# A batched matrix product: stores issued two at a time behind every second load of x

## The chip, the cores and the metric

The kernel runs on one core of a Trainium2 chip. A core has five engines that run at the same time and wait for one another by semaphores: PE (TensorE, matrix products), DVE (VectorE), ACT (ScalarE), POOL (GpSimd) and SP (SyncE). Sixteen DMA engines move data between the chip's main memory (DRAM) and the core's working memory; DMAs issued by POOL go to one queue (q0 below), those issued by SP to another (q1). The metric is the time of one execution in microseconds (us). "Span" is the time from the first to the last instruction in a profiled execution.

## The reference

```
batch, m, k, n = 32, 512, 1024, 768
x:      (batch, m, k)  float32
weight: (batch, k, n)  float32
out = np.matmul(x, weight).astype(np.float32)      # (32, 512, 768)
```

Thirty-two independent products of a 512x1024 and a 1024x768 matrix. 168 MB are read and 50 MB written.

## The kernel before

The batches go two by two: 16 pairs (`PAIRS`). Both inputs are cast to bf16 by the DMA that loads them, except for the first x, which SP loads as it is. For every pair k there are these pieces of work:

- **load of x**, x(k) (`load_x`, L108 to L111): 4 MB read, into one of two buffers. POOL first waits until the first quarter batch of products of pair k-2 is done, since the buffer is then free.
- **load of weights**, w(k) (`load_w`, L93 to L102): 6 MB read, both batches with one DMA, into one of two pairs of slots. POOL first waits until all products of pair k-2 are done. The last two batches (30 and 31) are loaded one by one, each behind its own wait.
- **transposes on PE** (L174): x has to be turned so that its columns lie on the partitions. Two bf16 numbers are turned at a time, as one float32; VectorE copies the result out of the accumulator (L220).
- **products on PE** (L166 and L139): per batch four quarters of 128 rows, each of 8 steps with two products. Before a pair's products PE waits for the weights (L178, by the word that SP passes on in `landed`).
- **copies out** of the accumulators by ACT (L262, L266) and VectorE (L271, L273) into one of four out slots (`OUT_SLOTS`). Two sets of accumulators take turns. Before the first copy of pair a, ACT waits in `slot_free` (L231 to L234) until the store of pair a-4 has landed, and passes that word on to VectorE. PE needs the first copies of a batch before its fourth quarter.
- **store**, s(a) (`store`, L117 to L119): 3 MB written. POOL first waits until all copies of pair a are done. The last two pairs are stored by SP: s(14) with one DMA, pair 15 in four half stores (L124).

What sets the order of the transfers is POOL's list, written out in `on_pool`. POOL works through it in order, so an issue stands behind the waits of everything ahead of it; and the queue q0 carries out what is issued in that order. After the first loads, turn k of the loop (k from 0 to 13) issues x(k+2), then s(k-2), then w(k+2). The last two of POOL's stores, s(12) and s(13), follow the loop.

Of the kernel before, what the change touches and what calls it, by code (L numbers as in the profile page):

```python
# [12 lines left out]
def kernel(  # L13
# [16 lines left out]
    PAIRS = B // 2  # L30
    HELD = 2
    GROUPS = 2 * MT
    W_SLOTS, X_SLOTS, OUT_SLOTS = 4, 2, 4

    pe, dve, act, pool, sp = nc.tensor, nc.vector, nc.scalar, nc.gpsimd, nc.sync
# [25 lines left out]
    def sem(name):  # L61
        sems.append(nc.alloc_semaphore(name))
        return sems[-1]
# [8 lines left out]
    s_st = [sem(f"s_st{i}") for i in range(OUT_SLOTS)]  # L72
# [3 lines left out]
    def mm_done(b):  # L76
        return 4 * (b + 1)
# [12 lines left out]
    def together(b):  # L90
        return W_SLOTS <= b < B - 2

    def load_w(b):  # L93
        if together(b):
            if b % 2 == 0:
                pool.wait_ge(s_mm, mm_done(b + 1 - W_SLOTS))
                slots = all_ws[:, b // 2 % 2].rearrange("p r ko n -> p r (ko n)")
                pool.dma_start(out=slots, in_=w_two_view[b // 2]).then_inc(s_w[b % W_SLOTS], 16)  # L98
            return
        if b >= W_SLOTS:  # L100
            pool.wait_ge(s_mm, mm_done(b - W_SLOTS))
        pool.dma_start(out=ws[b % W_SLOTS], in_=w_view[b]).then_inc(s_w[b % W_SLOTS], 16)  # L102
# [5 lines left out]
    def load_x(k):  # L108
        if k >= X_SLOTS:
            pool.wait_ge(s_mm, mm_begun(k - X_SLOTS))  # L110
        pool.dma_start(out=xs[k % X_SLOTS], in_=x_view[k]).then_inc(s_x[k % X_SLOTS], 16)  # L111

    def copied(eng, j):
        eng.wait_ge(s_ap, j + 1)
        eng.wait_ge(s_dp, j + 1)

    def store(eng, a, sem):  # L117
        copied(eng, 4 * a + 3)
        eng.dma_start(out=two_view[a], in_=outs[a % OUT_SLOTS]).then_inc(sem, 16)  # L119
# [222 lines left out]
    def on_pool():  # L342
        load_w(0)
        pool.memset(ident, 0.0).then_inc(s_zero, 1)  # L344
        pool.wait_ge(s_zero, 1)
        pool.affine_select(  # L346
            out=ident,
            in_=ident,
            compare_op=mybir.AluOpType.not_equal,
            fill=1.0,  # L350
            base=0,
            pattern=[[-1, P]],
            channel_multiplier=1,
        ).then_inc(s_ident, 1)
        load_w(1)
        load_x(1)
        load_w(2)
        load_w(3)
        for k in range(PAIRS - 2):
            load_x(k + 2)  # L360
            if k >= 2:
                store(pool, k - 2, s_st[(k - 2) % OUT_SLOTS])
            load_w(2 * k + 4)
            load_w(2 * k + 5)
        for a in range(PAIRS - 2 - HELD, PAIRS - 2):
            store(pool, a, s_st[a % OUT_SLOTS])

    def on_sp():
        for b in range(B):
# [18 lines left out]
    with tc.tile_critical(sync_engine=mybir.EngineType.Activation, no_gpsimd_drain=True):  # L388
        sp.dma_start(x_first, x_view[0]).then_inc(s_first, 16)
        on_pool()  # L390
        on_pe()
        on_dve()
        on_act()
        on_sp()
        clear_on_pool()
# [30 lines left out]
```

## Time and profile before

| | |
|---|---|
| median of 3 runs | 514.0 us (513.78 to 514.5) |
| the profiled execution's own time | 513.18 us |
| its span | 511.1 us |
| PE busy | 433.1 us, 85% |
| DVE / ACT / POOL busy | 42% / 23% / 6% |
| q0 (POOL's DMAs), share of the 16 engines' span | 95.5% |
| q1 (SP's DMAs) | 5.0% |
| DRAM read and written | 167.77 MB and 50.33 MB, 427 GB/s over the span |
| mean granted clock of PE | 0.955 |

How to read a profile: a row of the groups or of the timeline gives the line of the kernel, the engine, the operation and, as `out<-in`, what it writes and reads. A row of the waits has the waiting engine, tile and line, an arrow, what ended the wait, and then the total in us, how often, and the longest. In the timeline the first two numbers are start and duration in us, and in brackets stands the idle time of the engine before it and what ended that. In the slices, each digit is the busy share of a fortieth of the span in tenths. The windows view gives for each stretch of time the busy time of PE, PE's weight loads, DVE, ACT and POOL, then the granted clock of PE, the mean busy share of the DMA engines, and what they moved in GB/s. The trace also has a record of every packet that a DMA engine moved: its start, duration and size.

### The profile page before, as it was taken

To read this page: it belongs to the slowest core of one execution; us is meant where nothing else is said; L and a number is where in the kernel's file an instruction comes from. 1 tells how busy PE (TensorE), PEld (TensorE's weight loads), DVE (VectorE), ACT (ScalarE), POOL (GpSimd) and SP (SyncE) were. 2 spreads that over 40 slices of the span, in tenths; PEclk is the share of its full clock that TensorE was granted. 3 is DMA by queue.
4 is the path that set the end of the run, shared out by engine and by line. 5 is a ranking of instruction groups with operands and counts; after the bars stand their busy time and mean duration, and the time that the engine had idled before them with its cause. 6 is when DMAs were issued, how large, how long until landed. Compare 5 with 4: busy or idle time off the path is not lost. (4 is left out here: it accounts for less than half of the span.)

```text
span 511.1 us, 5831 instructions
## 1 busy us (share of the span) xinstructions
PE 433.1 (85%) x2560; PEld 174.0 (34%) x1536; DVE 212.9 (42%) x332; ACT 116.4 (23%) x197; POOL 29.1 (6%) x54
## 2 busy tenths in 40 slices
PE   0299999999998986969989599896998969889990
PEld 0143435252524341342433324233242333423420
DVE  0343636454536352352443535335353353623631
ACT  1313131313231311302223031130322303123130
POOL 2000001010100000000000000000000001000000
PEclk9999999999999998988999799897998989989996
DMA  8999999999999999999999999999999999999997
GB/s 296 263 210 215 223 213 215 219 299 248 224 330 224 318 231 222 334 223 335 215 237 318 219 337 217 253 304 219 336 215 265 291 222 334 220 272 279 344 435 296
DMA packets 9443, 136.34 MB, mean 267 GB/s; under 512 B 864, under 2 KB 864, under 8 KB 1376
## 3 DMA queue, kind: packets, MB, share of 16 engines
q0 software_dynamic: 8576, 125.83, 95.5%
q1 hardware_dynamic: 864, 10.49, 5.0%
q14 instruction: 3, 0.02, 0.0%
HBM read 167.77 MB, written 50.33 MB: 427 GB/s over the span
## 5 line engine op out<-in xcount | busy, mean ns | idle before, releaser
L166 PE MATMUL pm<-w,xT 128*128 x1024 | 349.1, 392 | 31.8 <-PEq L178 29.5
L139 PE MATMUL pm<-w,xT 128*128 x1024 | 286.2, 279 | 0.0
L166 PEld LDWEIGHTS pm<-w,xT 128*128 128x128 bf16 x1024 | 102.8, 100 | 275.0 <-issue 274.4
L271 DVE COPY outs<-pm 64x512 f32<-64x512 f32 x128 | 88.2, 689 | 200.8 <-DVEq L269 199.4
L262 ACT COPY outs<-pm 64x512 f32<-64x512 f32 x128 | 74.2, 580 | 267.2 <-PE pm L139 266.4
L174 PE MATMUL pt<-ident,x 128*128 128x128 f32 x512 | 84.9, 309 | 33.0 <-PEq L178 22.8
L220 DVE COPY xT<-pt 128x1024 bf16<-128x1024 bf16 x120 | 77.7, 687 | 63.8 <-PE pt L174 63.5
L174 PEld LDWEIGHTS pt<-ident,x 128*128 128x128 f32 x512 | 71.5, 210 | 48.4 <-issue 26.2
L266 ACT COPY outs<-pm 64x512 f32<-64x512 f32 x64 | 37.0, 579 | 97.7 <-PE pm L139 97.7
L273 DVE COPY outs<-pm 64x512 f32<-64x512 f32 x64 | 43.9, 686 | 0.0
L98 POOL DMA_DIRECT2D w<-in_weight_dram x13 | 9.2, 706 | 224.6 <-PE pm L139 224.6
L111 POOL DMA_DIRECT2D x<-in_x_dram x15 | 8.3, 555 | 170.0 <-PE pm L139 147.0
L281 DVE CAST x<-outs 128x1024 bf16<-128x1024 f32 x4 | 2.5, 688 | 18.5 <-DMA outs<-in_x_dram 18.5
L119 POOL DMA_DIRECT2D out_dram<-outs x14 | 7.5, 539 | 8.0 <-DVE outs L273 7.7
L281 ACT CAST x<-outs 128x1024 bf16<-128x1024 f32 x4 | 3.9, 1041 | 16.2 <-DMA outs<-in_x_dram 16.2
L228 DVE COPY xT<-pt 128x512 bf16<-128x512 bf16 x16 | 5.7, 417 | 4.1 <-PE pt L174 4.1
L102 POOL DMA_DIRECT2D w<-in_weight_dram x6 | 3.4, 566 | 17.4 <-PE pm L139 16.2
L281 ACT ACT_TABLE_LOAD x1 | 1.3, 1283 | 1.0 <-ACTq L388 1.0
L346 POOL TENSOR_SCALAR_AFFINE_SELECT ident<-ident 128x128 f32<-128x128 f32 x1 | 0.3, 284 | 0.2 <-POOL ident L344 0.2
L344 POOL MEMSET ident<- 128x128 f32 x1 | 0.2, 225 | 0.0
L410 POOL MEMSET const-float32-0.0<- 128x1 f32 x1 | 0.1, 99 | 0.2 <-issue 0.2
L410 POOL MEMSET const-bfloat16-1.0<- 128x1 bf16 x1 | 0.1, 103 | 0.0
(2 smaller groups left out, 0.2 us busy)
## 6 DMA issues: line engine op xcount, KB each, us to landing
out_dram<-outs POOLq DMA_DIRECT2D x14, 3072.0 KB, 43.2
w<-in_weight_dram POOLq DMA_DIRECT2D x13, 3072.0 KB, 39.2
x<-in_x_dram POOLq DMA_DIRECT2D x15, 2048.0 KB, 35.9
w<-in_weight_dram POOLq DMA_DIRECT2D x6, 1536.0 KB, 40.5
outs<-in_x_dram SPq DMA_DIRECT2D x1, 4096.0 KB, 17.6
out_dram<-outs SPq DMA_DIRECT2D x1, 3072.0 KB, 18.7
out_dram<-outs SPq DMA_DIRECT2D x4, 768.0 KB, 14.1
```

The lines of the kernel that those rows point to most:

```text
L98: pool.dma_start(out=slots, in_=w_two_view[b // 2]).then_inc(s_w[b % W_SLOTS], 16)
L111: pool.dma_start(out=xs[k % X_SLOTS], in_=x_view[k]).then_inc(s_x[k % X_SLOTS], 16)
L119: eng.dma_start(out=two_view[a], in_=outs[a % OUT_SLOTS]).then_inc(sem, 16)
L139: return pe.add_instruction(mybir.InstMatmult(name=nc.get_next_instruction_name(), engine=mybir.EngineType.PE, ins=[pe.lower_ap(moving), p ...
L166: last = pe.matmul(*args, start=(ko == 0), stop=(ko == KT - 1))
L174: last = pe.transpose(pts[g % 2][:, j, :], words[:, mo, j::JT], ident)
L220: return dve.tensor_copy(both[g // 2][:, :, :, g % 2].rearrange("p b j i r -> p j b i r"), pt)
L262: last = act.copy(*piece)
L266: act.copy(*pieces(b, p, 2)[0]).then_inc(s_ap, 1)
L271: last = dve.tensor_copy(*piece)
L273: dve.tensor_copy(*pieces(b, p, 2)[1]).then_inc(s_dp, 1)
L281: last = copy(xs[0][:, mo], x_first[:, mo])
```

## The change

In POOL's loop the store of one pair per turn becomes two stores in every second turn. In turn k, if k is even, s(k-3) and s(k-2) follow x(k+2); if k is odd, no store is issued. Turn 2 issues s(0) alone, turns 4, 6, 8, 10 and 12 issue s(1) and s(2), s(3) and s(4), and so on to s(9) and s(10). What is left after the loop, s(11), s(12) and s(13), is issued behind the last weight loads. So every even store keeps its place, and every odd one is issued one turn later; s(11) moves from turn 13 to behind w(30) and w(31). Nothing else is changed: not the waits in `store`, not the four out slots, not the stores of the last two pairs on SP.

```
+        def stores(first, last):
+            for a in range(max(first, 0), last):
+                store(pool, a, s_st[a % OUT_SLOTS])
+
+
         for k in range(PAIRS - 2):
             load_x(k + 2)
-            if k >= 2:
-                store(pool, k - 2, s_st[(k - 2) % OUT_SLOTS])
+            if k % 2 == 0:
+                stores(k - 3, k - 1)
             load_w(2 * k + 4)
             load_w(2 * k + 5)
-        for a in range(PAIRS - 2 - HELD, PAIRS - 2):
-            store(pool, a, s_st[a % OUT_SLOTS])
+        stores(PAIRS - 3 - HELD, PAIRS - 2)
```

## The prediction

> Below, pair k is batches 2k and 2k+1 (k from 0 to 15); x(k), w(k) and s(k) are its load of x, its load of weights and its store. Results are for the profiled execution: it took 513.18 us, 2.1 more than its span of 511.1, and lies 0.8 under the median of 514.0.
>
> **What bounds the kernel now.** I read the slices first, then the queues, the waits, the issue times, and the last microseconds.
>
> ```profile
> span 511.1 us, 5831 instructions
> ...
> DMA  8999999999999999999999999999999999999997
> ...
> q0 software_dynamic: 8576, 125.83, 95.5%
> q1 hardware_dynamic: 864, 10.49, 5.0%
> ```
>
> The 16 DMA engines are busy in every slice, and the two queues' packets add up to the whole span. TensorE is busy for 85%. What it waits for:
>
> ```profile
> ACT outs L262 <- PE pm L139: 266.4, 64, 14.7
> ...
> PE pm L166 <- PEq L178: 29.5, 9, 4.9
> ```
>
> L178 is the wait for a weight load: nine pairs stand up to 4.9 us before their first product. ACT's copies wait for TensorE alone: no row has them waiting for a store, so the wait for a free out slot is never felt. One turn of GpSimd's issues, and the landing of each (issue rows of windows around it: 36.0 us for x, 42.8 for the store, 39.2 for the weights):
>
> ```profile
> 359.21 0.56 POOL L111 DMA_DIRECT2D x<-in_x_dram  x1 [13.62 <-PE pm L139]
> 359.76 0.54 POOL L119 DMA_DIRECT2D out_dram<-outs  x1
> 377.74 0.71 POOL L98 DMA_DIRECT2D w<-in_weight_dram  x1 [17.44 <-PE pm L139]
> ```
>
> A transfer lands some 40 us after its issue, longer than a turn of 31.5: the queue is never empty, and a transfer lands when all before it have. The end, by windows (last three columns: clock, DMA share, GB/s):
>
> ```profile
> 504.00:507.00 3.00, 0.00 (x0) 0.00 (x0) 0.00 (x0) 0.00 (x0) 0.00 (x0) 0.50 1.02 426
> 507.00:508.00 1.00, 0.00 (x0) 0.00 (x0) 0.00 (x0) 0.00 (x0) 0.00 (x0) 0.50 0.46 191
> 508.00:509.00 1.00, 0.00 (x0) 0.00 (x0) 0.00 (x0) 0.00 (x0) 0.00 (x0) 0.50 0.16 68
> 509.00:510.00 1.00, 0.00 (x0) 0.00 (x0) 0.00 (x0) 0.00 (x0) 0.00 (x0) 0.50 0.07 31
> ```
>
> Most engines are out of work at 507.4; two or three run on to 509.8. The last store lands at 510.17, and the span ends there. So 505 us are packets back to back, and 2.4 us are the lateness of the last engine.
>
> **The change, part by part.** *The bytes.* None change. The trace's packet records carry sixteen 4-byte marks behind each transfer, one per DMA engine. Between the marks' medians a weight pair takes 14.52 us, x 9.69, a store 7.28; a weight pair behind x (no store between, in the first turns) takes 14.53, and x is 9.69 behind either. So a change of direction costs the typical engine 0.01 us, and removing some gains nothing there. Sum: 0.
>
> *GpSimd's issues.* The same 14 stores at 0.54 us, 15 x at 0.56, 13 pairs at 0.71. At even k GpSimd issues two stores behind x (0.54 more before it turns to the wait for the weights' slot, in which it sits 17 us); at odd k none. The store's own wait is for copies of pair k-2, done long before. Queued at most: x, w, x, s, s, against x, s, w, x, s now, the same packets. Sum: 0.
>
> *Stores s(1), s(3) ... s(11) land later.* An odd store goes out one turn later, behind one x and one weight pair: 9.69 + 14.52 = 24.2 us. Who waits: pair k+4's first copy on ACT (the slot), and behind it VectorE and TensorE. The turn of k = 12, in today's times with the new order: w(12) lands at 385.0; then x(13) 394.7, w(13) 409.2, x(14) 418.9, s(9) 426.2, s(10) 433.5, w(14) 448.0. Pair 13 needs the slot of s(9). Its transposes end at 413.7, the weights are there, so it starts at 413.8 (now 417.4). TensorE can do three quarters of the first batch (2.61 us each) into the free banks, to 421.7. The fourth needs the first copies: 426.2, then two ACT copies of 0.58, two VectorE copies of 0.69 and 0.4 for hand-overs, 429.1. That is a new wait of 7.4 us on TensorE, in pairs 5, 7, 9, 11 and 13. Behind it five quarters, 13.1 us, and up to 1.7 because the clock is low after a pause (granted 0.65 in the first 4.6 us of pair 12), then 5.8 of transposes: ready at 448.0 to 449.7, and w(14) lands at 448.0. So the wait uses up the wait for weights that stands there now, and pair 14 is 0 to 1.7 late. That doesn't add up over turns: the next odd pair's release is set by the DMA queue again.
>
> *Does the queue run dry?* w(15) is issued when pair 13 ends, 442 to 444; before it stand x(14) to w(14) and x(15), to 457.7: cover 13 to 15 us (now 24.8). Elsewhere 20 or more. Sum: 0.
>
> *The end.* s(11) moves behind the last two weight loads, which land 7.3 us earlier (466 and 473). Nothing comes of it: pair 15 starts at 477.0 when its transposes end, not at its weights (473.6). Its slot is that of s(11), landing at 481; the fourth quarter wants its copies at 484.9, and has them at 483.9. At 481 two stores are left on the queue, as now. The last half store, issued at 500.19, may slip by 4 us before the engines would idle for it (0.75 MB at 1.85 us, some 1.2 from issue to first packet, must start by 505.5). Sum: 0.
>
> *The late engines.* Here I expect the effect. The marks show how far the last engine is behind the first: 0.63 us at the first store, 0.67 at 172 us, 0.85 at 267, 1.30 at 361, 1.85 at 393, 2.77 at 456. It grows only where x gives way to a store: the late engine still reads its last packet of x while the others write, and that packet took 1.77 us at 393 and 2.14 at 455 instead of 1.23. Twelve such turns now; with the change six, and s(11) behind weights. Eight of the eleven turns after the first cost it 0.01 to 0.9, in proportion to its lateness (about 14% a turn). Five instead of eleven: 0.63 grows to about 1.2 instead of 2.77. A second engine loses 0.107 in every store, whatever the order, and ends 2.06 behind the bulk; without half of its hits some 1.7. So the end is 507.4 + 1.7 instead of 509.8: 0.7 us gained if that engine holds all else, 2.4 at most if all lateness goes, and a loss only if a hit is larger behind longer runs of writes, which no row shows. Unprofiled runs spread over 0.7 us and lie 0.8 above the profiled one; if that is more lateness of the growing kind, more is saved. I take 1.2, between 0.7 and that 1.5.
>
> The Trainium skill (DMA: Bandwidth & Descriptors, Latency and other measured facts) says that DMA engines 7 and 15 are usually slower, and gives as a best guess that all engines fetch the descriptors of GpSimd's DMAs through their ports. By that rule lateness would follow the number of descriptors and not the order, and the change would gain 0. The trace agrees for the second engine (0.107 per store throughout), not for the last one, which loses nothing in weights and in most stores.
>
> Total: 513.18 - 1.2 = 512.0 profiled; 514.0 - 1.2 = 512.8 as a median.
>
> **The rivals.**
> *No change.* Lateness has its own causes (the 0.107 per store), or is drawn anew in each run. For it: three of the eleven turns cost nothing, and one engine lost 0.42 at 333 us beside a fetch of instructions. Against it: each larger loss lies at a turn from x to a store. Time 514.0.
> *Slower: the slot wait reaches the end.* The wait of 7.4 us in five odd pairs is hidden only because TensorE now waits for weights. For it: TensorE is granted 0.65 after each pause, and ready and landing fall together within 2 us. Against it: a late TensorE lets no engine idle until it is 13 us late (w(15)'s cover) or the last half store 4 us. It decides from there; if the 1.7 of low clock carried over in all five pairs, 8.5 less 4 is 4.5 us: 518.5; with the cover of the end alone missed by 1, 515.
> *The stores don't pair up.* If GpSimd were held between the two, they would be apart; but both need copies a turn old, and sit 0.54 us apart. Nothing speaks for it; time 514.0.
>
> **How the numbers follow.** A time within 0.2% (1.03 us) can't be told from no change. Lateness shrinks: 0.62, of which 0.48 gains over 1.03 us and 0.14 less. No change (both kinds): 0.16. Slower: 0.22. The likeliest is faster, 512.8, its own range 511.6 (all 2.4 us gone) to 513.5. The range to the other cases: 511.6 to 515.3, which leaves out about 0.1 at the slow end and little below. Faster 0.48, same 0.30, slower 0.22.
>
> **What would show it.** Right: DMA at 9 in all slices; a row of ACT's copies waiting for out_dram some five times, 9 us each, near 166, 226, 289, 352 and 417 us; the waits for weights gone from every second pair; marks spread by less than 1.9 us at 470 us; the DMA share falling to nothing by 509. Wrong: a share under 0.9 before 500 us (the queue ran dry), the last half store issued after 504, or engines as late as now.

## The result and the profile after

The changed kernel takes 511.91 us (median of six runs, 511.72 to 512.37), against 514.04 for the kernel before in the same comparison (513.61 to 514.5). The ratio is 0.9962, with a 95% interval of 0.9952 to 0.9972: 2.1 us or 0.4% faster. The profiled execution took 512.11 us with a span of 510.1, so 2.0 us lie outside the span, as before. Against the profiled execution of the kernel before (513.18) that is 1.07 us less.

The page of the changed kernel, its slices and queues:

```profile
span 510.1 us, 5783 instructions
...
DMA  8999999999999999999999999999999999999997
...
q0 software_dynamic: 8576, 125.83, 95.7%
q1 hardware_dynamic: 864, 10.49, 5.0%
```

Bytes and packets are those of before, and the DMA engines are busy in every slice: the queue never ran dry. POOL's issues in turns 12 and 13, from the timeline:

```profile
388.29 0.56 POOL L111 DMA_DIRECT2D x<-in_x_dram  x1 [7.72 <-DVE outs L273]
388.85 1.06 POOL L119 DMA_DIRECT2D out_dram<-outs  x2
406.49 0.71 POOL L98 DMA_DIRECT2D w<-in_weight_dram  x1 [16.58 <-PE pm L139]
414.77 0.56 POOL L111 DMA_DIRECT2D x<-in_x_dram  x1 [7.58 <-PE pm L139]
```

Two stores now stand behind one x, and none behind the next. What this does to the engines, from the waits:

```profile
ACT outs L262 <- DMA out_dram<-outs: 100.2, 6, 19.2
...
PE pm L166 <- DVE outs L271: 36.3, 5, 8.2
...
PE pt L174 <- PEq L178: 23.1, 1, 23.1
```

The first row is new: ACT waits six times for a store to land. The second stood at one wait of 2.3 us before: now TensorE waits five times for the copies behind it, 7.3 us each on average. The third is the wait for the first x at the start; the nine waits for weights that stood under L178 before (29.5 us) are gone. So by these rows TensorE waits some 5 us longer than before, and for something else; the end of the kernel is not moved by it. The last microseconds of the changed kernel, in windows (last three columns: clock, DMA share, GB/s):

```profile
504.00:507.00 3.00, 0.00 (x0) 0.00 (x0) 0.00 (x0) 0.00 (x0) 0.00 (x0) 0.50 1.01 422
507.00:508.00 1.00, 0.00 (x0) 0.00 (x0) 0.00 (x0) 0.00 (x0) 0.00 (x0) 0.50 0.62 258
508.00:509.00 1.00, 0.00 (x0) 0.00 (x0) 0.00 (x0) 0.00 (x0) 0.00 (x0) 0.50 0.05 18
509.00:510.00 1.00, 0.00 (x0) 0.00 (x0) 0.00 (x0) 0.00 (x0) 0.00 (x0) 0.50 0.00 0
```

Here is the gain. Most engines finish in the same microsecond as before, on average a little later (0.62 of the share is left in 507 to 508, where it was 0.46), but in 508 to 509 only a share of 0.05 is left, where it was 0.16, and behind 509 nothing, where it was 0.07. The last packet of a store ends at 508.74 instead of 509.83, and the last store lands at 509.21 instead of 510.17. In the packet records the spread of the sixteen marks (one for each DMA engine) behind the last weight load, from the first engine to the last, is 0.74 us instead of 2.77.

### The profile page after: what moved, and what is told of

The parts are those of the page before. It is cut to its first block, busy times and chain, and to the rows that moved or that the text cites. A ratio compares the mean times of both kernels' runs of the same rounds, so it can differ in the third digit from the quotient of the medians.

```text
span 510.1 us, 5783 instructions
## 1 busy us (share of the span) xinstructions
PE 422.5 (83%) x2512; PEld 172.3 (34%) x1536; DVE 212.8 (42%) x332; ACT 115.8 (23%) x197; POOL 29.0 (6%) x54
## 3 DMA queue, kind: packets, MB, share of 16 engines
q0 software_dynamic: 8576, 125.83, 95.7%
## 5 line engine op out<-in xcount | busy, mean ns | idle before, releaser
L166 PE MATMUL pm<-w,xT 128*128 x976 | 328.2, 386 | 36.3 <-DVE outs L271 36.3
L139 PE MATMUL pm<-w,xT 128*128 x1024 | 283.9, 277 | 4.7 <-DVE xT L220 1.7
L262 ACT COPY outs<-pm 64x512 f32<-64x512 f32 x128 | 74.1, 579 | 264.1 <-PE pm L139 163.2
```

The costliest lines, as they stand in the source:

```text
L139: return pe.add_instruction(mybir.InstMatmult(name=nc.get_next_instruction_name(), engine=mybir.EngineType.PE, ins=[pe.lower_ap(moving), p ...
L166: last = pe.matmul(*args, start=(ko == 0), stop=(ko == KT - 1))
L262: last = act.copy(*piece)
```

## The experiments

All kernels of this table move the same bytes, and all but the last keep the DMA engines busy up to the last stores. The table gives the median, the ratio to the kernel before on the same chip, and, from the one profiled execution of each, its own time, the spread of the marks behind the last weight load, and the landing of the last store (all in us).

| kernel | median | ratio (95% interval) | profiled | spread | last landing |
|---|---|---|---|---|---|
| before, first trace | 514.0 | | 513.18 | 2.77 | 510.17 |
| before, again | 514.34 | 0.9998 (0.9990 to 1.0007) | 514.92 | 3.73 | 512.23 |
| changed, first trace | 511.91 | 0.9962 (0.9952 to 0.9972) | 512.11 | 0.74 | 509.21 |
| changed, again | 512.01 | 0.9963 (0.9950 to 0.9976) | 512.01 | 1.06 | 509.01 |
| single stores, one turn older | 513.63 | 0.9991 (0.9982 to 1.0000) | 514.51 | 4.09 | 511.51 |
| single stores ahead of x | 513.67 | 0.9990 (0.9981 to 0.9998) | 513.14 | 2.84 | 510.46 |
| halves together | 516.56 | 1.0057 (1.0042 to 1.0071) | 515.97 | 4.67 | 512.97 |
| halves apart | 514.31 | 1.0013 (1.0004 to 1.0022) | 513.87 | 2.98 | 511.19 |
| pairs ahead of x, even turns | 514.08 | 1.0012 (1.0004 to 1.0021) | 514.08 | 2.73 | 511.08 |
| pairs ahead of x, odd turns | 514.09 | 1.0004 (0.9995 to 1.0013) | 513.75 | 2.93 | 510.95 |
| pairs behind x, odd turns | 511.90 | 0.9965 (0.9953 to 0.9976) | 511.91 | 0.88 | 508.91 |
| before, with quiet turns | 513.56 | 0.9988 (0.9976 to 1.0000) | 513.27 | 2.95 | 510.59 |
| changed, VectorE kept busy | 515.12 | 1.0020 (1.0007 to 1.0033) | 514.77 | 1.61 | 509.30 |

(For the halves together the spread is that behind the last weight load but one; behind the last, the marks of two transfers overlap.) Over all rows but the last, the profiled time follows the spread: 511.9 to 512.1 at 0.7 to 1.1 us, 513.1 to 514.9 at 2.7 to 4.1, 516.0 at 4.7. The spread is not all of it: in three rows all engines end later too. From 507 to 508 the DMA share is 1.01 in "before, again", 0.97 in "halves together" and 0.92 in "halves apart", and 0.27 to 0.71 in the other rows but the last, which is explained below. Single executions scatter: of the 15 of "changed, again" and "pairs behind x, odd turns", two took 513.4 and 513.7 us, so the medians count, not one run.

### Is the lateness the same in every run?

The kernel before and the changed one, unchanged, on another occasion.

> The kernel before, once more, for its lateness. The number read is the spread of the sixteen marks (first to last DMA engine) behind the last weight load, at 474 us. Theory T (lateness grows at turns from x to a store, by their number): 1.5 to 3.5 us, as in the first trace (2.77), and 514.0 us. Rival N (lateness is drawn anew in each run, whatever the order): anywhere from 0.6 to 2.8.

> The changed kernel, once more. Theory T: with six turns from x to a store the spread of the marks behind the last weight load is 0.6 to 1.4 us, and the time 511.9. Rival N: the spread is anywhere from 0.6 to 2.8, and as often over 1.5 as in the kernel before.

The kernel before has a spread of 3.73 us, a little over what theory T allowed, the changed one of 1.06. The end of the kernel before, in windows:

```profile
507.00:508.00 1.00, 0.00 (x0) 0.00 (x0) 0.00 (x0) 0.00 (x0) 0.00 (x0) 0.50 1.01 424
508.00:509.00 1.00, 0.00 (x0) 0.00 (x0) 0.00 (x0) 0.00 (x0) 0.00 (x0) 0.50 0.68 283
509.00:510.00 1.00, 0.00 (x0) 0.00 (x0) 0.00 (x0) 0.00 (x0) 0.00 (x0) 0.50 0.31 129
510.00:511.00 1.00, 0.00 (x0) 0.00 (x0) 0.00 (x0) 0.00 (x0) 0.00 (x0) 0.50 0.13 55
511.00:512.00 1.00, 0.00 (x0) 0.00 (x0) 0.00 (x0) 0.00 (x0) 0.00 (x0) 0.50 0.04 18
```

The share fades over four microseconds, and this execution took 514.92. The one first traced, 513.18, was early for this kernel. But only part of the difference is the last engine: up to 508 all sixteen are still at work here, and behind the first 46 transfers the median mark stands at 479.71 us, where it is at 478.05 to 478.51 in every other trace of the table that has whole stores. So all engines lost some 1.4 us in this execution, and no record says to what. The spread is free of that. Rival N falls: two traces have 2.77 and 3.73, two 0.74 and 1.06, so the lateness of the last engine belongs to the order of the transfers, with a scatter of 0.3 to 1 us.

### Later stores, or fewer turns?

Store k-3 instead of k-2, one in every turn, so that every store is as late as the odd ones after the change:

```
-            if k >= 2:
-                store(pool, k - 2, s_st[(k - 2) % OUT_SLOTS])
+            if k >= 3:
+                store(pool, k - 3, s_st[(k - 3) % OUT_SLOTS])
...
-    HELD = 2
+    HELD = 3
```

> One store in every turn as before, but that of pair k-3, so each store is as late as the odd ones are after the change and there are eleven turns from x to a store with one store each; the end of the list is that of the changed kernel. Theory T (the number of turns counts): the spread at the last weight load is 1.5 us or more, the time 513.5 to 514.0. Rival P (what counts is which store stands beside which x, or when it is issued): the spread stays under 1.0 and the time is 511.9. Both: TensorE waits some 7 us for the out slot in nearly every pair, and this costs nothing at the end; if it cost, the time would be over 515.

513.63 us and a spread of 4.09. ACT now waits for the slot in eleven pairs:

```profile
ACT outs L262 <- DMA out_dram<-outs: 156.6, 11, 15.7
```

and the kernel isn't slower for it. So the wait for a slot costs nothing at the end, and a later store is not what gains: rival P falls.

Then the single store ahead of x(k+2) instead of behind it:

```
+            if k >= 2:
+                store(pool, k - 2, s_st[(k - 2) % OUT_SLOTS])
             load_x(k + 2)
-            if k >= 2:
-                store(pool, k - 2, s_st[(k - 2) % OUT_SLOTS])
```

> One store in every turn, that of pair k-2 as before, but issued ahead of x(k+2) instead of behind it: twelve turns, each from weights to a store and from the store to x. Theory T in its wide form (every turn from reading to writing counts): spread 1.5 us or more, 513.5 to 514.0 us. In its narrow form (only the last packet of x suffers, since its packets are the longest, 1.23 us against 0.93 for weights): spread under 1.2, 511.9 to 512.4 us. Rival N: anything.

513.67 us, spread 2.84: theory T in its wide form. The lateness now grows in the last packets of the weights, so it is not x that matters: any load that gives way to a store can do it. Here TensorE was idle most of the time at the turns (0 to 1.6 us busy in the 2 to 4 us around each, from the one at 195 us on), so its work is not needed for it either.

### More turns

Each of GpSimd's stores as two halves of the columns (and the waits for them counted in 32), once both where the store was, once the second one behind the weights:

```
+    def store_part(a, h, sem):
+        part = slice(h * ROW, (h + 1) * ROW)
+        pool.dma_start(out=two_view[a][:, part], in_=outs[a % OUT_SLOTS][:, part]).then_inc(sem, 16)
...
             load_x(k + 2)
             if k >= 2:
-                store(pool, k - 2, s_st[(k - 2) % OUT_SLOTS])
+                copied(pool, 4 * (k - 2) + 3)
+                store_part(k - 2, 0, s_st[(k - 2) % OUT_SLOTS])
+                store_part(k - 2, 1, s_st[(k - 2) % OUT_SLOTS])
```

and apart, against the halves together:

```
                 store_part(k - 2, 0, s_st[(k - 2) % OUT_SLOTS])
-                store_part(k - 2, 1, s_st[(k - 2) % OUT_SLOTS])
             load_w(2 * k + 4)
             load_w(2 * k + 5)
+            if k >= 2:
+                store_part(k - 2, 1, s_st[(k - 2) % OUT_SLOTS])
```

> The kernel before with each of GpSimd's stores cut into two DMAs of half the columns (12 KB a packet instead of 24), both issued where the store was: as many turns between loading and storing as before, twice the DMAs and packets of stores. Theory T (turns): spread of the marks behind the last weight load 1.5 to 4 us, time 513.5 to 514.5 us. Rival D (the number of DMAs or packets of stores is what makes engines late): spread over 5 us, time over 516.

> The same halves, but the second one is issued behind the weights instead of behind the first: 24 turns from loading to storing instead of 12, with the same bytes, DMAs and packets as with both halves together. Theory T: lateness grows by some 14% at a turn, so with twice the turns the spread is over 5 us and the time over 516 us. Rival D: the time is that of both halves together, within 0.5 us.

Both expectations missed. The halves together took 516.56 us (spread 4.67), the halves apart, with twice the turns, 514.31 (spread 2.98). In the trace of the halves apart the spread climbs to 2.76 by 222 us, in the first eight turns, and gains only 0.2 in the sixteen behind them. So theory T, in which each turn adds its share, is wrong as a count: lateness grows quickly and then stays for long. Smaller packets or more DMAs do cost all engines something: two halves take some 7.32 us between the median marks, where a whole store takes 7.27, and in both kernels the typical engine ends later (DMA shares of 0.97 and 0.92 in 507 to 508, against 0.46). What makes the last engine later still in the first of the two and not in the second, these runs don't tell.

### Pairs in another place

The changed kernel's two stores ahead of x(k+2), in the even turns:

```
-            load_x(k + 2)
             if k % 2 == 0:
                 stores(k - 3, k - 1)
+            load_x(k + 2)
```

> The changed kernel with its two stores issued ahead of x(k+2) in every even turn instead of behind it: the same number of turns, and the odd stores land 9.7 us earlier, so that TensorE's wait for the out slot (5 to 8 us in five pairs of the changed kernel) should all but go. Theory H (that wait is hidden by the DMA queue): 511.9 us, the same as the changed kernel within 0.5. Rival W (the wait costs something at the end): 1 us or more faster than the changed kernel, under 511.

514.08 us: neither theory. The wait for the slot is nearly gone, and TensorE again waits for weights, as these rows show:

```profile
PE pm L139 <- PEq L178: 40.9, 5, 9.0
...
ACT outs L262 <- DMA out_dram<-outs: 16.3, 2, 8.3
```

But the end is that of the kernel before:

```profile
507.00:508.00 1.00, 0.00 (x0) 0.00 (x0) 0.00 (x0) 0.00 (x0) 0.00 (x0) 0.50 0.48 197
508.00:509.00 1.00, 0.00 (x0) 0.00 (x0) 0.00 (x0) 0.00 (x0) 0.00 (x0) 0.50 0.12 49
509.00:510.00 1.00, 0.00 (x0) 0.00 (x0) 0.00 (x0) 0.00 (x0) 0.00 (x0) 0.50 0.12 49
510.00:511.00 1.00, 0.00 (x0) 0.00 (x0) 0.00 (x0) 0.00 (x0) 0.00 (x0) 0.50 0.03 12
```

With as few turns as the changed kernel, the spread is 2.73. The packet records show two late engines: one is hit at turns from weights to a store (0.2 to 0.8 us each), the other loses 0.13 to 0.25 in nearly every store, over packets of 0.93 to 0.98 us instead of 0.91.

To see whether the place or the even turns make the difference, the same two kernels with the pairs in the odd turns (`if k % 2:`, and two stores left at the end instead of three):

> The changed kernel with the pairs of stores in the odd turns instead of the even ones, behind x(k+2) again: s(0) and s(1) in turn 3, s(2) and s(3) in turn 5, and so on to s(10) and s(11) in turn 13; six turns from x to stores. Theory T (the number of turns counts, each adds to the lateness): spread behind the last weight load 0.6 to 1.7 us, time 511.9 to 512.4 us, as in the changed kernel. Rival C (the changed kernel only happens to have quiet addresses or moments in its even turns): spread over 2 us, time over 513.3.

> The same odd turns, with the two stores issued ahead of x(k+2), so that they follow weights. Pairs ahead of x in the even turns gave 514.1 us and a spread of 2.7 with as few turns as the changed kernel. If the place does it (a pair of stores behind weights makes engines late, a pair behind x doesn't): spread over 2 us, time over 513.3. If theory T is right and the even-turn kernel was the odd one out: spread under 1.7, time 511.9 to 512.4.

Behind x: 511.90 us, spread 0.88. Ahead of x: 514.09, spread 2.93. The end of the kernel with pairs behind x in odd turns:

```profile
507.00:508.00 1.00, 0.00 (x0) 0.00 (x0) 0.00 (x0) 0.00 (x0) 0.00 (x0) 0.50 0.27 111
508.00:509.00 1.00, 0.00 (x0) 0.00 (x0) 0.00 (x0) 0.00 (x0) 0.00 (x0) 0.50 0.02 6
```

So even or odd turns don't matter, and rival C falls. Pairs of stores behind x gain 2 us; pairs behind weights gain nothing. In the three traces with pairs behind x (both of the changed kernel, and this one) the spread did not rise at any of the turns from x to stores, behind the first, but for one (0.16 us at 417 us). What rise there is, 0.1 to 0.6 over the whole run, lies mostly beside a fetch of instructions, at the end, or in the second store of a pair.

### Are the copies beside a turn the cause?

In the changed kernel ACT and VectorE stand still when x gives way to the stores, because the slot isn't free. So a theory of its own, V: the copies beside a turn make the engines late. Two tests. First the kernel before, with ACT (and VectorE behind it) held until x(k+1) has landed:

```
         if b % 2 == 0 and p == 0:
             slot_free(b // 2)
+            k = b // 2
+            if 4 <= k < PAIRS - 1:
+                act.wait_ge(s_x[(k + 1) % X_SLOTS], 16 * ((k + 2) // 2))
```

> The kernel before, its order of transfers untouched (twelve turns from x to a store), with one wait more: in pairs 4 to 14 ACT starts its copies out only when x(k+1) has landed, so that ACT and VectorE copy nothing while the DMA engines turn from x to a store. Theory V (the copies of VectorE and ACT beside a turn are what makes the late engines later; the changed kernel gains because its wait for the out slot silences both at each turn): the spread of the marks behind the last weight load is under 1.2 us, and the time 511.9 to 512.4 us. Rival T (the number of turns counts): the spread is 1.5 to 4 us and the time 513.5 to 514.5.

The wait is there, in eleven pairs (the added lines move L262 to L265), and ACT and VectorE copy nothing at the ten turns from 173 us on:

```profile
ACT outs L265 <- DMA x<-in_x_dram: 160.1, 11, 16.3
```

and yet the spread grows at seven of these ten, to 2.95, and the time is 513.56. Second, the changed kernel with spare copies on VectorE in that quiet stretch:

```
+        def extra():
+            with dve.If_ne(turn, 0):
+                for i in range(EXTRA):
+                    part = spare[H * (i % 2):H * (i % 2 + 1), i // 2 * 512:(i // 2 + 1) * 512]
+                    dve.tensor_copy(part, pts[0].rearrange("p j c -> p (j c)")[0:H])
```

> The changed kernel, its order of transfers untouched, with twelve spare copies (accumulator bank to a spare tile, 64x512, 0.69 us each, 8 us in all) on VectorE in the odd pairs from pair 5 on, in the stretch in which it waits for the out slot. Theory V: the late engines grow later again at the turns from x to a store; spread at the last weight load 1.5 us or more, time 513 us or more. Rival T, or the order alone: the spread stays under 1.1 and the time is 511.9 to 512.3 (the spare copies end about when the slot comes free, so TensorE loses 2 us at most, and that is hidden).

VectorE was busy through all five turns. The spread was 1.25 at 456 us and 1.61 behind the last weights, more than in the changed kernel and just over the 1.5 that was expected of V. But only 0.3 us of it came at the five turns together, and 0.36 with the last weight load. So V falls as the cause by the first test, in which nothing was copied and the lateness grew all the same; that copies beside a turn add a few tenths isn't excluded by the second.

The time of 515.12 is another matter, and so is the last landing. In the last pair the spare copies hold up VectorE's first copies out until 486.36 (481.42 in the changed kernel). The last half store is then issued at 505.35 instead of 499.10, and the DMA engines run empty before it:

```profile
505.00:506.00 1.00, 0.00 (x0) 0.00 (x0) 0.28 (x1) 0.00 (x0) 0.00 (x0) 0.85 0.38 154
...
508.00:509.00 1.00, 0.00 (x0) 0.00 (x0) 0.00 (x0) 0.00 (x0) 0.00 (x0) 0.50 0.08 31
...
512.00:513.00 1.00, 0.00 (x0) 0.00 (x0) 0.00 (x0) 0.00 (x0) 0.00 (x0) 0.50 0.03 8
```

The pause lets the late engines catch up, so the landing at 509.30 says nothing of the lateness ahead of it. Behind the last store come one more packet of 8 KB, in the last line, and one of 16 KB, both on queues of instructions. The execution took 514.77 with a span of 510.2: 4.6 us outside the span, and all twelve of this kernel lie 4.4 to 4.9 outside, where the changed kernel has 2.0. Whether the packets or the longer program do this isn't shown: the trace of pairs ahead of x in odd turns has a packet of 16 KB behind its last store too, and 1.9 us outside its span.

### Where the wait for a slot does cost

The changed kernel with its pairs one turn older:

```
             if k % 2 == 0:
-                stores(k - 3, k - 1)
+                stores(k - 4, k - 2)
...
-        stores(PAIRS - 3 - HELD, PAIRS - 2)
+        stores(PAIRS - 4 - HELD, PAIRS - 2)
```

> The changed kernel with the two stores of an even turn taken one pair older (k-4 and k-3): the wait for the out slot comes in the even pairs, which start right as the queue takes up the transfers ahead of that store, and lasts some 30 us instead of 7. The weights of pair k+2 are then issued some 10 us after the queue is empty. By the working of the prediction (the wait is free until weights are issued more than 13 us late): the DMA engines idle 10 to 12 us in every second turn and the time is 570 to 600 us. Rival: if the wait were free whatever its length, 512.

607.17 us, ratio 1.1808 (1.1784 to 1.1832), a little over what was expected. The slices of the page, and the waits:

```profile
DMA  9999999999956989839899298992899955999954
```

```profile
ACT outs L262 <- DMA out_dram<-outs: 202.4, 6, 37.2
...
PE pm L166 <- DVE outs L271: 135.3, 6, 26.0
```

TensorE's wait is 26 us a time at most instead of 8, the weights behind it are issued after the queue has emptied, and the engines idle: in the packet records, from 255 to 266 and from 334 to 345 us, some 12 us in every second turn, with shorter gaps between. The cover that the prediction worked out is real; the changed kernel stays inside it.

## Why the prediction was right or wrong

The direction and its seat were right: 512.8 us was predicted and 511.91 measured, within the likeliest case's own range, and the gain is where it was put, in the lateness of the last DMA engine.

- **No gain for the typical engine.** Right: q0's share is 95.7% and the bulk of the engines ends in the same microsecond, 507 to 508.
- **GpSimd's issues.** Right: two stores take 1.06 us, and no wait stands between them. That the stores don't pair up was no issue.
- **The wait for the slot.** Right in size and place. 7.4 us in each of five pairs was worked out; the trace has 36.3 in five. Pair 13 was to end at 442 to 444, and its last product ends at 443.5; pair 14 was to start up to 1.7 us behind its weights, landed at 447.7, and starts at 449.3. ACT's own waits are longer than the 9 us announced (100.2 in six, up to 19.2), since they count from its last copy, and the sixth is that of pair 15.
- **The queue doesn't run dry, and the end has room.** Right: a share of 9 in all slices, and the last half store issued at 499.10, a microsecond earlier than before.
- **The late engines: the step that was mis-sized and, in its reasoning, wrong.** In the profiled executions the gain was 1.07 us, near the 1.2 taken; in the medians it was 2.1. Two things bear on that. The lateness of the changed kernel was put at 1.7 us behind the bulk; in its trace the last packet of a store ends at 508.74, 1.3 behind the 507.4 of the prediction (1.1 behind the typical engine, which ends at 507.63 here), and the spread at 456 us is 0.75 instead of 1.2. And the first trace of the kernel before was an early one: the same kernel again had a spread of 3.73, not 2.77, and took 1.7 us more, most of it because all engines were later. The prediction had allowed for more in the medians (0.8 us above the first trace), but no row could tell; how much of the 2.1 us is the last engine's lateness in the executions without a trace isn't known.
- **Its reasoning**, 14% of lateness a turn whatever stands around it, did not hold. Pairs ahead of x have as few turns and spreads of 2.7 and 2.9; twice the turns gave 3.0. That the count came near the spread here (1.2 for 0.75) is in part luck: for pairs ahead of x it would have given the same time, and these took 514.1. The engine said to lose 0.107 us in every store, whatever the order, did not: in the changed kernel's trace no engine loses anything in the first store of a pair behind x, but for 0.1 us in s(9), beside a fetch of instructions. The best guess of the Trainium skill (DMA: Bandwidth & Descriptors, Latency and other measured facts) that was weighed there, engines made late by the fetching of descriptors, would have left the time as it was; with as many DMAs and packets as before (8576 packets on q0) the spread fell to 0.74. Which engines are the late ones no record says.

What is shown: the time follows the lateness of the last engine at the end; the order of loads and stores sets that lateness; and of the orders tried, only two stores behind x keep it under 1.7 us, in even turns and in odd ones. What is excluded as the cause: how late a store is, the number of turns alone, the copies of ACT and VectorE beside a turn (as the main cause), and the wait for the slot alone (single stores with that wait in eleven pairs have a spread of 4.09). What stays open is why a pair behind x leaves the engines together while a pair behind weights doesn't. The two differ in one thing more: pairs behind x come with TensorE's wait for the slot, and pairs ahead of x nearly without. At the turn itself TensorE works through in the changed kernel (busy for 1.70 of the 1.70 us around the turn at 417.8) and begins to wait only at 419.7, while the first store runs; whether that wait helps then is not shown. An out slot more would separate the two; it takes 24 KB more in each partition and wasn't tried.

## What to carry to other kernels

Where the DMA engines are busy from end to end, look at the last microseconds by windows: bytes set when the typical engine ends, and the slowest of the sixteen sets the time; here it ended 1 to 4 us behind the typical one. The order in which loads and stores are queued moves that lateness without moving a byte, but not by a rule as simple as counting the changes of direction, so an order has to be timed. A new wait of 7 us on a busy engine can be free when it takes the place of another wait; work out up to which point it is, since one turn more cost 95 us here.

## What the runs showed that was not expected

- The first store of a run makes all engines late at once: in the kernel before, the x ahead of it takes 0.44 us longer than the others (10.13 instead of 9.69 between the marks, on average over the engines). Where the first store comes a turn later, this moves with it (to 133 us, and is 0.1 to 0.2 us there), and where it comes behind weights, the weights pay 0.3 to 0.5. Later turns don't do that to all engines, with few exceptions.
- An engine that is late stays late. In the four traces of the kernel before and the changed one the spread never shrank by more than 0.2 us from one mark to the next up to 478 us, so a loss of 0.1 us early on is still there at the end.
- A late engine's packets can be hit hard: the last packet of x took up to 2.14 us instead of 1.23 at the turn in the kernel before, while packets in the middle of a load took what they always take.
